# Retention gate columns between the v convolution and the last v transposes, q's norms taken at its convolution, v copied unscaled

## The chip, the cores and the metric

The kernel runs on one core of one Trainium2 chip. The metric is the device time of one execution in microseconds, as the median of several runs. Five engines work beside each other, each through its own list of instructions in order: TensorE (PE; its weight loads are shown apart as PEld), VectorE (DVE), ScalarE (ACT), GpSimd (POOL) and SyncE (SP), which does nothing but issue transfers. ACT issues transfers as well (shown as ACTq). An instruction that waits holds up all that stand behind it on its engine.

## What is computed

One layer of a diffusion backbone on 1024 latent tokens and 256 context tokens, model width 1024. An adaLN-modulated RMSNorm is followed by one input projection, whose columns feed two mixers: a bidirectional gated DeltaNet with four heads and a centred short convolution on q, k and v, and a bidirectional retention with four heads. Their gated outputs go through one output projection and a SwiGLU. The parts that the change touches:

```python
def l2_normalize(t):
    return t * lax.rsqrt(jnp.sum(t * t, axis=-1, keepdims=True) + NORM_EPS)
...
    qkv_a, z, ab, rq, rk, rv, rg = jnp.split(p, splits, axis=-1)
    qkv_a = jnp.concatenate([short_conv(qkv_a[:, :CTX_LEN], cw), short_conv(qkv_a[:, CTX_LEN:], cw)], axis=1)
    q, k, v = [t.reshape(b, tl, N_HEADS_GDN, HEAD_DIM) for t in jnp.split(qkv_a, 3, axis=-1)]
    q = l2_normalize(q) * (HEAD_DIM ** -0.5)
    k = l2_normalize(k)
...
    o_f = gated_delta_rule(q, k, v, g_f, jax.nn.sigmoid(b_f))
...
    o_gdn = rms_norm(o_f + o_b, gdn_norm_g) * jax.nn.silu(z.reshape(b, tl, N_HEADS_GDN, HEAD_DIM))
...
    o_ret = head_group_norm(r_f + r_b, ret_norm_g) * jax.nn.silu(rg.reshape(b, tl, N_HEADS_RET, HEAD_DIM))
```

Inside `gated_delta_rule`, a triangular system with the matrix I + A is solved for each chunk and head, where A holds the products of k with k, times beta and the decay exp(G_i - G_j).

## The kernel before

**Number format.** Every large matmul is done as three: both operands are split into a high part (`whi`, `hhi`) and the rest (`wlo`, `hlo`), and hi·hi, hi·lo and lo·hi are added in one bank. For weights ACT makes `whi` (L344) and DVE or POOL `wlo` (L345).

**Token-major groups.** `token_major(g, ...)` multiplies the normed tokens with 256 columns of the input projection (`tm`, L371 to L373): for eight latent tiles 8 x 24 = 192 matmuls of 128x256. Groups 6 and 7 are the gate columns rg of the retention; their `finish` is `fin_gate`, a Silu on ACT (L532), and the result `res` is stored for later. Groups 8 and 9 are z. Each group has two pairs of split weights, which live in a pool: W2 for groups 6 and 7, W for z and for the convolutions.

**Convolutions.** `conv_block(b, y, lat)` computes one head of k, q or v, channel by token, in banks `b` (L611 to L613), copies the bank to `u` and, scaled, to `y` on ACT (L614, L615), adds the four shifted terms on DVE (L621), and ends with a Silu on ACT (L624). There are three buffers for `y`. Blocks 4 to 7 are k, 0 to 3 q, 8 to 11 v.

**k.** `kstat` (from L630) turns `y` into token-major tiles, sums the squares of each token into `nk`, takes a reciprocal of it, and stores two scaled copies. The decay row `grow_d`, which the pair stage broadcasts, is turned (`GT`, L595) and stored ahead of the k convolutions.

**Row sums.** `ada_rest(5, h)`, called in the first two convolutions of q, accumulates eight products of adaLN weights (`adaw`, loaded in four transfers into two buffers) in `acc` on DVE (L497, L499), sums them over partitions with one matmul on PE (`gr`, L504), adds the bias (`row`, L505) and stores the row (`grow`, L506). It uses one `acc` and one `row`.

**Pair stage.** `pre(t)`, for each of ten tiles (L702 to L737): `kc` is loaded, PE makes `kk` (L705); for latent tiles `qc` is loaded and transposed (`qt`, L710), ACT sums the squares of each token into `nq` (L712), and PE makes `kq` (L715). For both directions the decay row is loaded (`gw`, L718), POOL masks it (`e`, L722), ACT takes four exps (L726), DVE multiplies into `ut` and `sp` (L730, L732), which are stored.

**Inversion and merge.** `invert(b)`, for batches of four, four and two tiles, loads the `ut` as `yr`, copies it to `L` (ACT L758 and DVE L759), does 31 dependent pairs of a product and a subtraction on DVE (`tmp` L765, `X` L767), and turns the result (`XT`, L769). `merge(b)` (`m`, L807 to L838) follows on PE.

**v.** After each v convolution ten transposes (`vT`, L856) go to three banks; ACT scales each 128x128 tile by a factor of its k norm (`vt`, L859, 40 in all), and stores it.

**Order.** The text of the program is ada and norms, token-major groups 0 and 1 (rv), k, q, gates (groups 6, 7), `solve(0)` and `solve(1)` (each `pre` for its tiles, then `invert`), v, `pre` for the last two tiles, merges, z, the scans, and later the rotary groups of the retention. A scheduler that simulates a timeline decides the order on each engine; so z groups and merges are mixed, and the v convolutions run among the pair stage.

Of the kernel before, what the change touches and what calls it, by code (L numbers as in the profile page):

```python
# [17 lines left out]
P = 128  # L18
D = 1024
KT = D // P  # L20
NCTX = 256
# [17 lines left out]
def build(nc, tc, ap, dbg=None, stop=None, marks=None):  # L39
# [151 lines left out]
    try:  # L191
# [402 lines left out]
        ps = bank_b("GT")  # L594
        T.transpose(ps[:80, :P], sm["G"], ident)  # L595
        gT = AB.tile([80, P], F32, tag="gT", name="gT")
        V.tensor_copy(gT, ps[:80, :P])
        SY.dma_start(grow_d, gT)
# [30 lines left out]
        a4, b4, kds4 = (sm[n].rearrange("p (t d h) -> p t d h", d=2, h=4) for n in ("ab", "beta", "kds"))  # L629

        def kstat(h, y):
# [9 lines left out]
            V.tensor_scalar(nk[:, :, h], nk[:, :, h], EPS, None, ALU.add)  # L641
            rk2 = R2.tile([P, TT], F32, tag="rk2", name="rk2", bufs=2)
            V.reciprocal(rk2, nk[:, :, h])
            V.tensor_tensor(a4[:, :, :, h], b4[:, :, :, h], bc(rk2, [P, TT, 2], 2), ALU.mult)
            V.tensor_tensor(kds4[:, :, :, h], kds4[:, :, :, h], a4[:, :, :, h], ALU.mult)
            for (t0, n), pt, kt in zip(cut, ps, kts):
# [21 lines left out]
        nkf = nk.rearrange("p t h -> p (t h)")  # L668

        lnk = log(GS, nkf, TT * H, "ln").rearrange("p (t h) -> p t h", h=H)  # L670
        nG4 = sm["nG"].rearrange("p (t d h) -> p t d h", d=2, h=H)
        V.tensor_tensor(lnb, lnb, bc(lnk, [P, TT, 2, H], 2), ALU.subtract)
# [12 lines left out]
        checkpoint("q")  # L685
        for g in (6, 7):
            token_major(g, LAT, fin_gate, S, W2, SY)
# [12 lines left out]
        def pre(t):  # L700
# [5 lines left out]
            if t >= 2:  # L706
                qc = load(GP, qd[t - 2], "qc", 2)
                pn = bank_b("qt")
                for h in range(H):
                    T.transpose(pn[:, h * P:(h + 1) * P], qc[:, h, :], ident)  # L710
                for h in range(H):
                    S.activation(pn[:, h * P:(h + 1) * P], pn[:, h * P:(h + 1) * P], AF.Square, accum_out=nq[:, t - 2, h:h + 1])  # L712
# [135 lines left out]
        solve(0)  # L848
        solve(1)
        for h in range(H):  # L850
            y = newy()
            conv_block(8 + h, y, False)
# [802 lines left out]
```

## Time and profile before

| what | us |
|---|---|
| median of three runs (1477.37 to 1480.02) | 1479.93 |
| the profiled execution | 1477.96 |
| span of its trace | 1476.2 |
| PE busy | 1397.2 |
| DVE busy | 964.6 |
| ACT busy | 614.0 |
| POOL busy | 590.3 |

The mean clock that was granted to TensorE is 0.983. The span is cut in stages by time below: a row of such a table gives from and to, the length, then the busy time of PE, PEld, DVE, ACT and POOL with the number of instructions in brackets, the granted clock (1.00 is full), the DMA share and GB/s. A row of a timeline gives the start, the length, the engine and the line with its operation, and in brackets the idle time before it and what ended it. A row of grouped instructions ends in busy time and mean ns of one, then the idle time of the engine just before them and its releasers. A row of waits gives the instruction that waited, what it waited for, the total in us, how often, and the longest.

### The profile page before, as it was taken

Reading aid. Unit: us, or ns where it says so; the run is one execution under the profiler, and the core shown is the slowest. Engines: PE = TensorE matmul, PEld = TensorE weight load, DVE = VectorE, ACT = ScalarE, POOL = GpSimd, SP = SyncE. Lnnn points to the kernel's source line nnn. Section 1 sums busy time; section 2 is a strip of 40 time slices with the busy share of each in tenths; the row PEclk is TensorE's granted clock in tenths of the full one; section 3 lists DMA queues with packets and bytes.
Section 4 is the critical chain, followed back from the end, with each engine's and each line's share of the span. In section 5 each row is a group of like instructions: output and inputs, shape, how many; then the busy total and the mean of one; then the engine's idle time right before and its main releaser. Section 6 shows DMA issues by size and latency. Waiting matters only on the chain.

```text
span 1476.2 us, 24111 instructions
## 1 busy us (share of the span) xinstructions
PE 1397.2 (95%) x8919; PEld 1199.2 (81%) x8919; DVE 964.6 (65%) x1856; ACT 614.0 (42%) x1326; POOL 590.3 (40%) x501
## 2 busy tenths in 40 slices
PE   7999999986789999899799899999999999999997
PEld 2898888975689999898688688877888888788885
DVE  6566789289792435689676877556555564657477
ACT  5643564587333111245443623233333332444445
POOL 0120010243202344234144688898555552335321
PEclk9999999998899999999899999999999999999999
DMA  9536686688888625996532265674222242776863
GB/s 337 197 105 205 189 249 200 219 264 277 282 216 277 238 76 178 416 341 209 184 125 104 97 238 210 242 264 162 105 97 105 107 151 79 260 260 194 288 216 114
DMA packets 170421, 298.14 MB, mean 202 GB/s; under 512 B 43496, under 2 KB 93880, under 8 KB 165952
## 3 DMA queue, kind: packets, MB, share of 16 engines
q1 hardware_dynamic: 118752, 253.17, 50.2%
q10 hardware_dynamic: 49072, 35.83, 7.8%
q0 software_dynamic: 2480, 7.60, 1.4%
q8 instruction: 70, 1.15, 0.3%
q14 instruction: 47, 0.39, 0.1%
HBM read 206.60 MB, written 89.96 MB: 201 GB/s over the span
## 4 chain that ended last, share of the span: by engine, by line
PE 55%; POOL 6%; DMA 5%; DVE 4%; issue 2%; ACT 2%; SPq 1%; ACTq 0%; POOLq 0%; DVEq 0%
PE ffn L1344 7%; PE ffn L1342 6%; PE ffn L1343 6%; PE fo L1470 4%; PE fo L1469 4%; PE fo L1468 4%; PE tm L371 3%; PE tm L373 3%; PE tm L372 3%; PE op L1203 2%; PE op L1201 2%; PE op L1202 2%; DMA wd<-tw 2%; POOL ws L1315 1%; DMA pk<-sd 1%
## 5 line engine op out<-in xcount | busy, mean ns | idle before, releaser
L371 PE MATMUL tm<-whi,hhi 128*128 128x256 f32 (+1 forms) x704 | 199.5, 287 | 7.7 <-ACT vt L859 3.4
L372 PE MATMUL tm<-wlo,hhi 128*128 128x256 f32 (+1 forms) x704 | 199.3, 285 | 2.4 <-issue 2.0
L373 PE MATMUL tm<-whi,hlo 128*128 128x256 f32 (+1 forms) x704 | 197.7, 285 | 0.0
L371 PEld LDWEIGHTS tm<-whi,hhi 128*128 128x128 f32 x704 | 132.8, 190 | 11.8 <-ACT vt L859 3.6
L1342 PE MATMUL ffn<-t,whi 128*128 128x512 f32 x352 | 136.9, 390 | 1.3 <-ACT whi L344 1.3
L1344 PE MATMUL ffn<-t,wlo 128*128 128x512 f32 x352 | 137.0, 390 | 1.0 <-DVE wlo L345 1.0
L1343 PE MATMUL ffn<-t,whi 128*128 128x512 f32 x352 | 137.0, 389 | 0.0
L372 PEld LDWEIGHTS tm<-wlo,hhi 128*128 128x128 f32 x704 | 133.7, 190 | 2.1 <-issue 0.9
L373 PEld LDWEIGHTS tm<-whi,hlo 128*128 128x128 f32 x704 | 132.8, 190 | 2.6 <-issue 1.8
L344 ACT ACTIVATE whi<-wraw 128x512 fp32r<-128x512 f32 (+2 forms) x98 | 75.1, 771 | 141.4 <-PE ffn L1343 80.5
L344 ACT ACTIVATE whi<-ws 128x512 fp32r<-128x512 f32 x88 | 55.6, 632 | 171.5 <-PE ffn L1343 123.4
L345 DVE TENSOR_TENSOR wlo<-ws,whi 128x512 fp32r<-128x512 f32 x88 | 93.9, 1068 | 47.0 <-ACT whi L344 46.8
L1469 PE MATMUL fo<-wlo,ahi 128*128 128x512 f32 x308 | 120.2, 390 | 2.1 <-DVE wlo L345 2.1
L1468 PE MATMUL fo<-whi,ahi 128*128 128x512 f32 x308 | 119.3, 390 | 0.7 <-ACT ahi L344 0.7
L1470 PE MATMUL fo<-whi,alo 128*128 128x512 f32 x308 | 119.0, 390 | 0.0
L345 DVE TENSOR_TENSOR wlo<-wraw,whi 128x512 fp32r<-128x512 f32 (+2 forms) x92 | 99.4, 1082 | 24.6 <-ACT whi L344 24.6
L1342 PE MATMUL ffn<-b,whi 128*128 128x512 f32 x264 | 103.8, 393 | 4.4 <-ACT whi L344 4.4
L1344 PE MATMUL ffn<-b,wlo 128*128 128x512 f32 x264 | 103.6, 393 | 0.8 <-DVE wlo L345 0.8
L1343 PE MATMUL ffn<-b,whi 128*128 128x512 f32 x264 | 103.4, 392 | 0.0
L612 PE MATMUL b<-hlo,whi 128*128 128x512 f32 (+1 forms) x256 | 94.4, 369 | 0.0
L613 PE MATMUL b<-hhi,wlo 128*128 128x512 f32 (+1 forms) x256 | 94.3, 368 | 0.0
L611 PE MATMUL b<-hhi,whi 128*128 128x512 f32 (+1 forms) x256 | 94.3, 368 | 0.0
(446 smaller groups left out, 3448.1 us busy)
## 6 DMA issues: line engine op xcount, KB each, us to landing
adaw<-ada SPq DMA_DIRECT2D x48, 512.0 KB, 4.4
pk<-sd SPq DMA_DIRECT2D x16, 1536.0 KB, 10.0
wraw<-wfi SPq DMA_DIRECT2D x44, 512.0 KB, 3.7
ar<-ad SPq DMA_DIRECT2D x33, 512.0 KB, 4.7
w<-wfo SPq DMA_DIRECT2D x22, 512.0 KB, 5.7
wd<-tw SPq DMA_DIRECT2D x11, 1024.0 KB, 4.8
ad<-act SPq DMA_DIRECT2D x20, 512.0 KB, 3.0
raw<-wd SPq DMA_DIRECT2D x20, 512.0 KB, 4.9
```

Source lines behind the costliest of these rows:

```text
L344: S.activation(hi, raw, AF.Copy)
L345: e.tensor_tensor(lo, raw, hi.bitcast(F32), ALU.subtract)
L371: T.matmul(o, hhi[:, k, tsl], whi[:, k % 4, :], start=(k == 0), stop=False)
L372: T.matmul(o, hhi[:, k, tsl], wlo[:, k % 4, :], start=False, stop=False)
L373: T.matmul(o, hlo[:, k, tsl], whi[:, k % 4, :], start=False, stop=(k == KT - 1))
L612: T.matmul(o, whi[:, k, :], hl, start=False, stop=False)
L1342: T.matmul(o, whi[:, k, :], xhi(xn, slice(0, 4), k), start=(first and k == 0), stop=False, **kw)
L1343: T.matmul(o, whi[:, k, :], xlo(xn, slice(0, 4), k), start=False, stop=False, **kw)
L1344: T.matmul(o, wlo[:, k, :], xhi(xn, slice(0, 4), k), start=False, stop=(k == 3), **kw)
L1468: T.matmul(po[g][i], ahi[:, ts], whi, start=(j == 0 and not kw), stop=False, **kw)
L1469: T.matmul(po[g][i], ahi[:, ts], wlo, start=False, stop=False, **kw)
L1470: T.matmul(po[g][i], alo[:, ts], whi, start=False, stop=(j == FH - 1), **kw)
```

## The change

Half of the rg columns (group 7) leave their place ahead of the pair stage and stand between the last v convolution and its transposes; their weights come from pool W. Each head's `vT` follows the next head's convolution (`vturn`), and the copies of v are plain, one for a bank. So that v needs no factor, the norms are arranged anew: `kstat` takes a rsqrt (`rk1`) where it took a reciprocal, and scales `neG` with it too; `grow_d` becomes G less half the log of the squared norm and moves behind that log; the rsqrt of all k norms (`sv`) goes; `rn`, the reciprocal of the squared k norms, enters the output gate with one more product. The squares of q are taken from `y` at the convolutions (`qstat`), no longer in `pre`.

```diff
@@ -595,5 @@
-        ps = bank_b("GT")
-        T.transpose(ps[:80, :P], sm["G"], ident)
-        gT = AB.tile([80, P], F32, tag="gT", name="gT")
-        V.tensor_copy(gT, ps[:80, :P])
-        SY.dma_start(grow_d, gT)
@@ kstat @@
-            V.tensor_scalar(nk[:, :, h], nk[:, :, h], EPS, None, ALU.add)
-            rk2 = R2.tile([P, TT], F32, tag="rk2", name="rk2", bufs=2)
-            V.reciprocal(rk2, nk[:, :, h])
-            V.tensor_tensor(a4[:, :, :, h], b4[:, :, :, h], bc(rk2, [P, TT, 2], 2), ALU.mult)
+            nkh = R2.tile([P, TT], F32, tag="nkh", name="nkh", bufs=2)
+            V.tensor_scalar(nkh, nk[:, :, h], EPS, None, ALU.add)
+            rk1 = rsqrt(R2, nkh, TT, "rk")
+            V.tensor_tensor(a4[:, :, :, h], b4[:, :, :, h], bc(rk1, [P, TT, 2], 2), ALU.mult)
             V.tensor_tensor(kds4[:, :, :, h], kds4[:, :, :, h], a4[:, :, :, h], ALU.mult)
+            V.tensor_tensor(neG4[:, :, :, h], neG4[:, :, :, h], bc(rk1, [P, TT, 2], 2), ALU.mult)
@@ k, q and gates @@
+        V.tensor_scalar(nkf, nkf, EPS, None, ALU.add)
         lnk = log(GS, nkf, TT * H, "ln").rearrange("p (t h) -> p t h", h=H)
+        V.tensor_scalar(lnk, lnk, 0.5, None, ALU.mult)
+        V.tensor_tensor(Gr, sm["G"].rearrange("p (t d h) -> p t d h", d=2, h=H), bc(lnk, [P, TT, 2, H], 2), ALU.subtract)
+        ps = bank_b("GT")
+        T.transpose(ps[:80, :P], Gr.rearrange("p t d h -> p (t d h)"), ident)
+        V.tensor_copy(gT, ps[:80, :P])
+        SY.dma_start(grow_d, gT)
...
-        sv = rsqrt(GS, nkf, TT * H, "sv")
-        V.tensor_tensor(sv, sv, nkf, ALU.mult)
-        sv3 = sv.rearrange("p (t h) -> p t h", h=H)
+        V.reciprocal(rn.rearrange("p t h -> p (t h)"), nkf)
+        def qstat(h, y):
+            for l0 in (0, 4):
+                pn = bank_b("qt")
+                for i in range(4):
+                    T.transpose(pn[:, i * P:(i + 1) * P], y[:, NCTX + (l0 + i) * P:NCTX + (l0 + i + 1) * P], ident)
+                for i in range(4):
+                    S.activation(pn[:, i * P:(i + 1) * P], pn[:, i * P:(i + 1) * P], AF.Square,
+                                 accum_out=nq[:, l0 + i, h:h + 1])
         for h in range(H):
             y = newy()
             conv_block(h, y, True)
...
+            qys.append(y)
+            if h:
+                qstat(h - 1, qys[h - 1])
-        for g in (6, 7):
-            token_major(g, LAT, fin_gate, S, W2, SY)
+        token_major(6, LAT, fin_gate, S, W2, SY)
+        qstat(H - 1, qys[H - 1])
@@ pre @@
-                pn = bank_b("qt")
-                for h in range(H):
-                    T.transpose(pn[:, h * P:(h + 1) * P], qc[:, h, :], ident)
-                for h in range(H):
-                    S.activation(pn[:, h * P:(h + 1) * P], pn[:, h * P:(h + 1) * P], AF.Square, accum_out=nq[:, t - 2, h:h + 1])
@@ v @@
+        def vturn(h, y):
             for t0, n in ((0, 2), (2, 4), (6, 4)):
...
-                for t in range(n):
-                    S.activation(vt[:, t], ps[:, t * P:(t + 1) * P], AF.Copy, scale=sv3[:, t0 + t, h:h + 1])
+                S.activation(vt[:, :n], ps[:, :n * P].rearrange("p (t j) -> p t j", j=P), AF.Copy)
...
+        for h in range(H):
+            ys.append(newy())
+            conv_block(8 + h, ys[h], False)
+            if h:
+                vturn(h - 1, ys[h - 1])
+        token_major(7, LAT, fin_gate, S, W)
+        vturn(H - 1, ys[H - 1])
@@ output gate @@
+            V.tensor_tensor(nqe, nqe, rn[:, l + 2, :], ALU.mult)
```

The order of the instructions changes with it; rows of the order now have the changed kernel's line numbers (`vT` L865, `kk` L723, `kq` L728, Silu of y L619, exps L739). On PE at the end of the q stage, the second row sum of `ada_rest` (`gr`, L504) stood 151 rows behind the first, among the matmuls of group 7. Its surroundings before:

```order
L612 MATMUL b_2376<-hlo,whi 128x512
L613 MATMUL b_2376<-hhi,wlo 128x512
L611 MATMUL b_2376<-hhi,whi 128x512
L504 MATMUL gr<-acc,ones 1x512
L612 MATMUL b_2376<-hlo,whi 128x512
...
L372 MATMUL tm<-wlo,hhi 128x256
L504 MATMUL gr<-acc,ones 1x512
L371 MATMUL tm<-whi,hhi 128x256
```

and now, on the same engine at the same place, behind the convolutions of q (`GT` is the turned decay row, `b_3374` the first bank of v):

```order
L673 MATMUL GT<-ident,Gr 80x128
L504 MATMUL gr<-acc,ones 1x512
L371 MATMUL tm<-whi,hhi 128x256
L372 MATMUL tm<-wlo,hhi 128x256
L373 MATMUL tm<-whi,hlo 128x256
...
L504 MATMUL gr<-acc,ones 1x512
L686 MATMUL qt<-ident,y 128x128 x16
L606 MATMUL b_3374<-hhi,whi 128x256
```

Between the two row sums stand nine matmuls of group 6 where 150 instructions stood, and behind the second come the transposes of q and then v without group 7.

On SP at the same place, the transfers between the two rows keep their order (`grow` are the stored rows, `adaw` and `row` the loads of the second sum, `kc` and `gw` those of the pair stage); `grow_d` is new there:

```order
L676 DMA grow_d<-gT 80x128
L506 DMA grow_1231<-row 1x512
L495 DMA adaw_2305<-ada 128x1024
L503 DMA row<-adarow 1x512
L495 DMA adaw_2309<-ada 128x1024
L506 DMA grow_1231<-row 1x512
L660 DMA kc<-sd 128x512
L731 DMA gw<-grow_d 128x512 x2
```

The loads of the pair stage thus stand behind both stored rows, as they did before, and now behind the decay row too.

On PE around the last ten `vT`, before:

```order
L613 MATMUL b_3980<-hhi,wlo 128x512
L705 MATMUL kk<-kc 128x128 x3
L856 MATMUL vT<-ident,y 128x128 x10
L705 MATMUL kk<-kc 128x128
L710 MATMUL qt<-ident,qc 128x128 x4
L715 MATMUL kq<-qc,kc 128x128 x4
...
L856 MATMUL vT<-ident,y 128x128 x10
L371 MATMUL tm<-whi,hhi 128x256
```

and now, from the last bank of v (`b_3766`) on, where the `tm` ahead of the last `vT` are those of group 7 (48, 120 and 24 in the three gaps) and the one behind it is the first of group 8:

```order
L608 MATMUL b_3766<-hhi,wlo 128x512
L865 MATMUL vT<-ident,y 128x128 x7
L728 MATMUL kq<-qc,kc 128x128 x4
L865 MATMUL vT<-ident,y 128x128 x3
L723 MATMUL kk<-kc 128x128 x4
L371 MATMUL tm<-whi,hhi 128x256
...
L728 MATMUL kq<-qc,kc 128x128 x4
L723 MATMUL kk<-kc 128x128
...
L723 MATMUL kk<-kc 128x128 x3
L728 MATMUL kq<-qc,kc 128x128 x4
...
L865 MATMUL vT<-ident,y 128x128 x10
L371 MATMUL tm<-whi,hhi 128x256
```

The last transposes stood right behind the pair matmuls of their time; now group 7 stands ahead of them. On ACT the Silu of group 7 (L532) and of v (L619) stand among the exps of the pair stage (L739), each with a load of its table where the function changes:

```order
L739 ACTIVATE e<-e,nG 128x128 x4
...
L532 ACT_TABLE_LOAD
L532 ACTIVATE res<-tm 128x256
...
L739 ACT_TABLE_LOAD
L739 ACTIVATE e<-e,nG 128x128 x4
...
L619 ACT_TABLE_LOAD
L619 ACTIVATE y<-y 128x1280
L532 ACTIVATE res<-tm 128x256
```

In the whole program the table loads on ACT go from 20 to 28.

More of the change, by code (lines that the diff above doesn't have):

```diff
@@ L627, in newy @@
             return CV.tile([P, NTOK], F32, tag="y", name="y", bufs=3)
-        a4, b4, kds4 = (sm[n].rearrange("p (t d h) -> p t d h", d=2, h=4) for n in ("ab", "beta", "kds"))
+        a4, b4, kds4, neG4 = (sm[n].rearrange("p (t d h) -> p t d h", d=2, h=4) for n in ("ab", "beta", "kds", "neG"))
         def kstat(h, y):
@@ L846, in solve @@
             checkpoint("inv%d" % b)
[L848 to L852, printed above, removed]
+        def vturn(h, y):
             for t0, n in ((0, 2), (2, 4), (6, 4)):
@@ L857, in build @@
                 vt = CV.tile([P, 4, P], F32, tag="vt", name="vt", bufs=2)
-                for t in range(n):
-                    S.activation(vt[:, t], ps[:, t * P:(t + 1) * P], AF.Copy, scale=sv3[:, t0 + t, h:h + 1])
+                S.activation(vt[:, :n], ps[:, :n * P].rearrange("p (t j) -> p t j", j=P), AF.Copy)
                 S.dma_start(vd[t0:t0 + n, :, h, :].rearrange("t p j -> p t j"), vt[:, :n])
+        solve(0)
+        solve(1)
+        ys = []
+        for h in range(H):
[5 more added lines that the diff above has]
+        vturn(H - 1, ys[H - 1])
         close(CV)
```

4 lines of the change are left out of this document (added).

## The prediction

> **What bounds the kernel now.** I read the shares of the engines first, then the busy time of each engine by stage, then TensorE's waits in the stages that the change touches.
>
> ```profile
> PE 1397.2 (95%) x8919; PEld 1199.2 (81%) x8919; DVE 964.6 (65%) x1856; ACT 614.0 (42%) x1326; POOL 590.3 (40%) x501
> ```
>
> TensorE (PE) is busy for 1397.2 of 1476.2 us. The change leaves the number and the size of its matmuls as they were, so it can win only from PE's 79 us of idle time and from its clock. Next the stages, as from:to, length, then the busy us of PE, weight load, DVE, ACT and POOL, the granted clock, the DMA share, GB/s:
>
> ```profile
> 220.00:262.00 42.00, 42.00 (x242) 35.24 (x241) 39.72 (x81) 18.06 (x44) 2.89 (x2) 1.00 0.62 195
> 262.00:276.00 14.00, 14.00 (x119) 13.94 (x118) 0.00 (x0) 6.56 (x14) 1.27 (x2) 1.00 0.63 189
> 276.00:310.00 34.00, 33.62 (x205) 29.00 (x205) 18.86 (x23) 25.68 (x69) 13.43 (x17) 1.00 0.80 255
> 310.00:375.00 65.00, 44.08 (x261) 37.88 (x259) 60.89 (x89) 54.08 (x155) 29.05 (x23) 0.90 0.84 265
> 375.00:416.00 41.00, 33.22 (x549) 32.21 (x550) 33.27 (x87) 12.30 (x28) 4.67 (x4) 0.96 0.92 271
> 490.00:580.00 90.00, 90.00 (x769) 89.85 (x768) 38.34 (x120) 9.84 (x12) 39.67 (x78) 1.00 0.42 155
> ```
>
> 220 to 276 (q convolutions and gate columns) and 490 to 580 are full. From 276 to 416 PE is idle for 0.4 + 20.9 + 7.8 = 29.1 us, while DVE has nothing at all to do from 262 to 276. This is a stage bound by DVE from 310 on (60.9 of 65) and by PE before it. Its waits, from 276 to 490 (total, times, longest):
>
> ```profile
> PE vT L856 <- ACT y L624: 9.6, 2, 9.3
> PE kk L705 <- issue: 8.4, 3, 6.7
> PE m L814 <- issue: 3.4, 2, 2.2
> PE tm L371 <- ACT vt L859: 3.4, 1, 3.4
> ```
>
> The three places at which group 7 and the plain copies can tell are the last transposes of v (9.3), the copies of v (3.4) and the pair stage (kk, 8.4). The row of the longest (start, length, x count, in brackets the idle time ahead of it and what ended it), an undisturbed one of the same ten transposes, and two rows of the clock, in the columns of the stages, show what it costs besides:
>
> ```profile
> 375.06 2.39 PE L856 MATMUL vT<-ident,y 128*128 128x128 f32 x10 [9.27 <-ACT y L624]
> 305.00 1.31 PE L856 MATMUL vT<-ident,y 128*128 128x128 f32 x10 [0.32 <-ACT y L624]
> ...
> 370.00:375.00 5.00, 0.00 (x0) 0.00 (x0) 5.00 (x7) 4.97 (x12) 3.36 (x2) 0.50 0.48 175
> 375.00:380.00 5.00, 4.95 (x29) 4.95 (x30) 4.52 (x15) 1.77 (x7) 1.18 (x1) 0.66 1.03 355
> ```
>
> In the 5 us after the wait 4.95 us of matmuls ran at 0.66, so about 4.95 x 0.34 = 1.7 us went to the clock. I put the loss of the whole stage (0.90 over 44.1 us of matmuls, part of it transposes) at 3 us. With the 3.4 us of m behind it, PE loses 29.1 + 3.4 + 3 = **35.5 us** here.
>
> **The change, part by part.**
>
> *Group 7's 192 matmuls move from 240–276 to between the v convolutions and the last vT.* They are 22.8 us (192 at the 0.12 us by which the starts of these rows follow each other):
>
> ```profile
> 378.50 0.28 PE L371 MATMUL tm<-whi,hhi 128*128 128x256 f32 x1
> 378.62 0.28 PE L372 MATMUL tm<-wlo,hhi 128*128 128x256 f32 x1
> ```
>
> They fill the 9.3 us ahead of the last vT and part of the 8.4 us at kk. But in their old place they filled something too, which is what is late next. The rows of the adaLN accumulation at the end of the q stage:
>
> ```profile
> 240.21 0.67 DVE L505 TENSOR_TENSOR row<-row,gr 1x512 f32<-1x512 f32 x1
> 243.93 0.33 SPq L495 DMA_DIRECT2D adaw<-ada  x1
> DMA to landing us min/median/max: 3.4/3.9/4.4
> 260.04 1.02 PE L504 MATMUL gr<-acc,ones 128*1 128x512 f32 x2
> 261.10 0.68 DVE L505 TENSOR_TENSOR row<-row,gr 1x512 f32<-1x512 f32 x1 [1.84 <-PE gr L504]
> ```
>
> Between the first row sum and the second lies a chain: SP issues the last weights (adaw) 243.93 - 240.21 = 3.7 us after the first row, behind a DMA that waits for that row; landing takes 3.9; two accumulations of 0.7 follow. That is 9.0 us. Before, some 20 us of matmuls stood between the two gr matmuls and PE did not notice. In the new order there are nine (1.1 us), so PE, which works in order, stands there for about 8.4 us (6 to 11: the ends of the landing row, and the transposition GT just ahead), and by the clock rows above loses 2 us more after it. The Trainium skill, "TensorE: Matmul & The Clock Gate", in its part on transposes, says that transposes do not count as busy for the clock; 16 of them follow this gap, and by that rule the loss would be nearer 3 us. The ten vT that took 2.39 us behind the long wait and 1.31 us elsewhere fit it, but do not prove it.
>
> Where is the second gr then? It was at 260.0 with about 65 of group 7's matmuls (7.7 us) done before it; those are gone and 8.4 us of standing take their place, so it stays at about 261. The kc loads of the pair stage are queued on SP behind the DMA of its row, and so the first ut stays near its old place, too. The v convolutions however now begin at 262 instead of 276, 13 us ahead.
>
> *The squares of q* (32 transposes and 32 squares) go from the pair stage to the q convolutions:
>
> ```profile
> L712 ACT ACTIVATE qt<-qt 128x128 f32<-128x128 f32 x32 | 8.7, 271 | 1.1 <-ACT qt L712 0.8
> L712 ACT ACTIVATION_READ_ACCUMULATOR qt<-qt 128x1 f32 x32 | 6.3, 196 | 0.0
> L710 PE MATMUL qt<-ident,qc 128*128 128x128 f32 x32 | 5.3, 294 | 2.6 <-issue 1.9 <-PE kk L705 0.7
> L859 ACT ACTIVATE vt<-vT,svy 128x128 f32<-128x128 f32 x40 | 11.3, 363 | 13.0 <-DMA sd<-vt 11.7 <-PE vT L856 1.3
> L614 ACT ACTIVATE u<-b 128x512 f32<-128x512 f32 x16 | 9.5, 595 | 5.5 <-PE gr L504 3.8 <-PE b L613 1.7
> L726 ACT ACT_TABLE_LOAD x5 | 6.4, 1283 | 0.9 <-ACT res L532 0.8
> ```
>
> 15.0 us leave ACT in the pair stage and fall into 240 to 280, where it has 24 of 42 us free. The last of them release a buffer of y and the banks of the v convolution, so the first ut may come up to 5.5 us later than 277.5; at nothing at the other end, I take **3 us**.
>
> *The copies of v*: 40 in 11.3 us become 12 of at most 0.6 us each (the 512-wide u<-b above): 11.3 - 7.2 = 4 us off ACT. The wait of 3.4 us that PE had for the last of them goes, as I take it; it stays at worst, since the copy still waits for the DMA that empties its buffer (the 11.7 us in its row).
>
> *More table loads.* The gates of group 7 (Silu) now stand between the exps of the pair stage, and the number of table loads in the program goes from 20 to 28: 8 x 1.283 = 10.3 us on ACT, against 15 + 4 us that left it. The group's eight stores are issued by ACT too, and its two weight loads move from SP's queue to ACT's: ten issues of 0.35 us, 3.5 us more there, and SP is freer by two. The neighbours of one table load show that 1.283 us is all of its price, and the last row is an issue:
>
> ```profile
> 323.89 0.62 ACT L735 ACTIVATE gw<-gw 128x512 f32<-128x512 f32 x1
> 324.52 1.28 ACT L624 ACT_TABLE_LOAD   x1
> 325.81 1.27 ACT L624 ACTIVATE y<-y 128x1280 f32<-128x1280 f32 x1
> 387.83 0.35 ACTq L387 DMA_DIRECT2D zd<-res  x1
> ```
>
> The Trainium skill, "ScalarE: Activation LUTs", section "What ACT_TABLE_LOAD costs", speaks against the change: it has 1283 ns for the load and 1380 ns for a drain, 2.66 us for a switch, and asks that functions be grouped by table set. By that price the eight would be 21 us. The trace agrees with the 1283 ns and shows no drain (0.01 us on either side).
>
> *Small operations of DVE* (a rsqrt for each head of k, Gr, rn, one more in each gate, against a rsqrt of 40 columns that goes) are some 45 more. At the length of a like one now that is 45 x 0.168 = 8 us, spread from the k convolutions to the row sums.
>
> ```profile
> L641 DVE TENSOR_SCALAR nk<-nk 128x10 f32<-128x10 f32 x2 | 0.3, 168 | 0.0
> ```
>
> DVE is busy for 39.7 of 42 us from 220 to 262, so their cover is PE's own full work there and the last y of q, which the new order puts behind the row sums. With the cover they cost nothing, which I take; without it the 8 us would come at GT, and the range has 3 of them.
>
> *Weights of z group 8.* Group 7 now holds the two buffers of the weights until its last matmul, and the low halves of group 8 stand on DVE around the copy XT(0). On PE the matmuls of group 8 come right behind the last vT.
>
> ```profile
> 277.48 1.29 DVE L730 TENSOR_TENSOR ut<-kk,e 128x512 f32<-128x512 f32 x2 [15.70 <-POOL X L755]
> 381.01 2.20 DVE L769 COPY XT<-X 128x1024 f32<-128x1024 f32 x1
> 374.11 0.68 DVE L732 TENSOR_TENSOR sp<-kq,e 128x512 f32<-128x512 f32 x1
> L730 DVE TENSOR_TENSOR ut<-kk,e 128x512 f32<-128x512 f32 x20 | 13.5, 685 | 30.9 <-POOL X L755 15.7 <-ACT e L726 7.0 <-DMA un<-ut 4.4
> 389.32 0.20 DVE L765 TENSOR_TENSOR tmp<-L,X 128x31 f32<-128x31 f32 x1 [5.03 <-ACT L L758]
> 404.21 0.58 PE L807 MATMUL m<-t,U 32*32 32x32 f32 x4
> 276.29 1.95 PE L705 MATMUL kk<-kc 128*128 128x128 f32 x16
> ```
>
> When is XT(0)? From the first ut to its end (277.5 to 383.2, 105.7 us) DVE worked 18.9 + 60.9 + 8.2 = 88 us. Its idle time before 310 waited for PE's convolutions, which are 13 us ahead now; I leave it only the 4.1 us of 310 to 375: 277.5 + 3 + 88.0 + 4.1 = **372.6**, 10.6 us sooner. When does PE reach the last vT? From 276.3 to 375.1 it worked 98.8 - 21.3 = 77.5 us; with 22.8 more for group 7, 5 less for the transposes of q, and 4 us of waits at kk (between none and the 8.4 of now; half), from 262 on: 361.3, and 363 with the vT. The low halves are there at about 370.4, ahead of the XT copy, so PE waits some **7.4 us** (1, if the halves were free to come at once).
>
> **The sum**, twice. On PE: 35.5 us lost before; after it 8.4 + 2 at the row sums, 4 at kk, 7.4 at group 8, 3.4 at m, together 25.2: a gain of 10.3. On DVE: XT(0) 10.6 us sooner; the merge began at 404.2, 21 us after it, and would begin at 393.6. From there on the work is as before. The profiled run took 1477.96 us (2 under the median, 1479.93), and so I say **1468**.
>
> **The rivals.**
>
> *More goes.* The waits at kk and for group 8 don't come (0 and 1), as the pair stage gets its operands earlier and its ACT is relieved by 19 - 10.3 - 3.5 = 5 us: 35.5 - 10.4 - 1 - 3.4 = 20.7 us, and 24 if the m waits go too: 1457 to 1454. For it: DVE's 14 idle us from 262. Against it: the first ut is where it was.
>
> *Nothing comes of it.* The pair stage has a pace of its own: its 20 steps ran from 277.5 to 374.8, 4.86 us each, through exp, select, product and DMA. If it keeps that, XT(0) comes 3 us later and the last vT's wait merely turns into one for the weights or at kk; the 5.0 us for L (ACT stood behind the DMA of the vt copies) are saved: about -2, **1476**. For it: POOL and DMA (0.84) had part in the pace. Against it: DVE was full from 310 on, with work that now comes sooner.
>
> *Slower.* The switches of tables lie in the path of the exps, each of which releases a ut: 3 + 10.3 - 5.0 = +8.3, **1486**. It decides as soon as what was added (10.3) isn't met by what left ACT in the same steps, so that the 10.9 us that ACT had free from 310 to 375 are used up; the order on ACT puts gates that wait for PE's group 7 ahead of exps, which is for it, and the 19 us that left are against it. With the page's 2.66 us it would be +19.
>
> **How the numbers follow.** My forecast (1462 to 1473) 0.45; more 0.17; nothing 0.14; slower 0.24, with the gap at the row sums at its upper end in it. 0.2%, about what a measurement of this kernel tells from no change, is 3 us: faster 0.62, same 0.14, slower 0.24. The range goes from 1450 (more, with the kk waits and clock all gone) to 1486.
>
> **What would show it.** Right: a PE wait of about 8 us at the second gr L504, ended by DVE's acc; no long wait ahead of the last vT; XT(0) near 373, merge near 394; eight more table loads of 1283 ns with ACT still under 60 of 65. Wrong: a first ut after 283, no wait at gr, ut waits for e of more than the 7 us of now, or a merge at or after 404.

## The result and the profile after

The changed kernel takes 1493.49 us (median, 1489.83 to 1495.77); the kernel before took 1479.88 us in the same comparison. The ratio is 1.0096, with a 95% interval of 1.0075 to 1.0117: 13.6 us slower, where 10 us faster was forecast. The profiled execution has a span of 1493.9 us against 1476.2.

The first row of the page after, to be held against that of before:

```profile
PE 1405.3 (94%) x8919; PEld 1206.9 (81%) x8919; DVE 978.4 (65%) x1900; ACT 619.7 (41%) x1306; POOL 592.9 (40%) x501
```

The same 8919 matmuls took 8.1 us more of PE's time (1405.3 against 1397.2), and PE was idle for 88.6 us instead of 79.0. Of the 17.7 us in the span, 9.6 are idle time and 8.1 the longer time of the same matmuls; the mean granted clock was 0.972 against 0.983. The stages, in the columns of the table of before:

```profile
220.00:262.00 42.00, 33.53 (x189) 27.17 (x187) 30.83 (x75) 16.35 (x56) 4.45 (x5) 0.88 0.66 200
276.00:310.00 34.00, 32.12 (x199) 29.00 (x198) 22.69 (x26) 25.54 (x65) 14.82 (x13) 0.95 0.83 267
310.00:375.00 65.00, 58.32 (x393) 52.81 (x392) 59.85 (x100) 49.31 (x95) 23.14 (x22) 0.97 0.87 270
375.00:416.00 41.00, 28.98 (x198) 27.90 (x198) 24.37 (x58) 11.81 (x19) 5.94 (x5) 0.79 0.86 267
416.00:490.00 74.00, 60.82 (x1373) 57.31 (x1371) 38.01 (x95) 22.52 (x42) 4.00 (x7) 0.86 0.67 186
```

The last of them had been nearly full before:

```profile
416.00:490.00 74.00, 70.56 (x1231) 67.71 (x1231) 38.92 (x106) 18.78 (x36) 12.55 (x25) 0.98 0.82 244
```

From 310 to 375 PE stood still for 6.7 us where it had stood for 20.9: this is the part that the change aimed at, and it worked. The idle time came back in three places: 8.5 us in 220 to 262, where there had been none, 12.0 instead of 7.8 in 375 to 416, and 13.2 instead of 3.4 in 416 to 490. In the last two the granted clock fell to 0.79 and 0.86. The waits of PE in 276 to 490, summed by line (us, count, longest):

```profile
PE tm L371 <- ACT res L532: 11.5, 3, 6.8
PE m L830 <- issue: 7.5, 2, 4.6
PE vT L865 <- ACT res L532: 5.1, 2, 4.2
```

and the one at the row sums, from PE's timeline:

```profile
256.69 1.86 PE L504 MATMUL gr<-acc,ones 128*1 128x512 f32 x2 [8.20 <-DVE acc L499]
```

The wait of 9.3 us ahead of the last vT is 4.2 now. That for the row sum is 8.20 us, where 8.4 was forecast. New are the waits for `res`; the merges' own (`m`) have grown from 4.3 us to 11.0.

What the merge waits for is seen on ACT, SP and DVE (start, length, engine, operation, count). After:

```profile
374.12 0.68 ACT L739 ACTIVATE e<-e,nG 128x128 f32<-128x128 f32 x2
374.82 1.28 ACT L532 ACT_TABLE_LOAD   x1
376.12 0.38 ACT L532 ACTIVATE res<-tm 128x256 f32<-128x256 f32 x1
376.52 1.28 ACT L739 ACT_TABLE_LOAD   x1
377.81 0.40 ACT L739 ACTIVATE e<-e,nG 128x128 f32<-128x128 f32 x1
378.30 0.69 DVE L743 TENSOR_TENSOR ut<-kk,e 128x512 f32<-128x512 f32 x1 [3.15 <-ACT e L739]
381.46 1.06 DVE L782 COPY XT<-X 128x1024 f32<-128x1024 f32 x1
392.87 2.94 SPq L796 DMA_DIRECT2D U<-un  x2
408.00 0.33 SPq L891 DMA_DIRECT2D rope<-rope  x1
408.42 4.83 SPq L801 DMA_DIRECT2D t<-xd  x4
417.13 0.25 PE L820 MATMUL m<-t,U 32*32 32x32 f32 x6
422.83 1.07 DVE L782 COPY XT<-X 128x1024 f32<-128x1024 f32 x1
426.85 0.67 DVE L823 TENSOR_SCALAR xt<-m 128x512 f32<-128x512 f32 x1
```

and the same places before:

```profile
375.45 0.51 SPq L783 DMA_DIRECT2D U<-un  x1
391.78 0.56 SPq L783 DMA_DIRECT2D U<-un  x1
393.59 10.27 SPq L788 DMA_DIRECT2D t<-xd  x4
409.58 0.68 DVE L810 TENSOR_SCALAR xt<-m 128x512 f32<-128x512 f32 x1
415.24 1.09 DVE L769 COPY XT<-X 128x1024 f32<-128x1024 f32 x1
```

XT of batch 0 stands where it stood (381.5 against 381.0), but the merge begins 12.9 us later (417.1 against 404.2). Two things differ. The two loads `U<-un` of 2 MB each left SP 16 us apart and now leave together, after XT; and `xt`, the first merge's negated copy, stood ahead of XT of batch 1 on DVE and now stands behind it.

### The profile page after: what moved, and what is told of

Same layout as the page of the kernel before. It is cut to its first block, busy times and chain, and to the rows that moved or that the text cites. A ratio compares the mean times of both kernels' runs of the same rounds, so it can differ in the third digit from the quotient of the medians.

```text
span 1493.9 us, 24143 instructions
## 1 busy us (share of the span) xinstructions
PE 1405.3 (94%) x8919; PEld 1206.9 (81%) x8919; DVE 978.4 (65%) x1900; ACT 619.7 (41%) x1306; POOL 592.9 (40%) x501
## 4 chain that ended last, share of the span: by engine, by line
PE 51%; DMA 8%; POOL 6%; DVE 5%; issue 3%; ACT 2%; SPq 0%; ACTq 0%; DVEq 0%; POOLq 0%
PE ffn L1364 6%; PE ffn L1363 6%; PE ffn L1362 6%; PE fo L1488 4%; PE fo L1490 4%; PE fo L1489 4%; PE tm L371 2%; PE tm L373 2%; PE tm L372 2%; PE op L1221 2%; PE op L1223 2%; PE op L1222 2%; POOL ws L1335 1%; DMA wd<-tw 1%; DMA w<-wfo 1%
## 5 line engine op out<-in xcount | busy, mean ns | idle before, releaser
L371 PE MATMUL tm<-whi,hhi 128*128 128x256 f32 (+1 forms) x704 | 203.8, 293 | 16.1 <-ACT res L532 11.5
L372 PE MATMUL tm<-wlo,hhi 128*128 128x256 f32 (+1 forms) x704 | 203.0, 290 | 0.5 <-DVE wlo L345 0.5
L373 PE MATMUL tm<-whi,hlo 128*128 128x256 f32 (+1 forms) x704 | 201.2, 290 | 0.0
L371 PEld LDWEIGHTS tm<-whi,hhi 128*128 128x128 f32 x704 | 136.8, 196 | 21.2 <-ACT res L532 12.2
L372 PEld LDWEIGHTS tm<-wlo,hhi 128*128 128x128 f32 x704 | 137.6, 195 | 2.2 <-issue 0.9
L373 PEld LDWEIGHTS tm<-whi,hlo 128*128 128x128 f32 x704 | 136.8, 196 | 0.7 <-DVE hlo L314 0.2
## 6 DMA issues: line engine op xcount, KB each, us to landing
pk<-sd SPq DMA_DIRECT2D x16, 1536.0 KB, 10.4
```

The costliest lines, as they stand in the source:

```text
L371: T.matmul(o, hhi[:, k, tsl], whi[:, k % 4, :], start=(k == 0), stop=False)
L372: T.matmul(o, hhi[:, k, tsl], wlo[:, k % 4, :], start=False, stop=False)
L373: T.matmul(o, hlo[:, k, tsl], whi[:, k % 4, :], start=False, stop=(k == KT - 1))
```

## The experiments

Each run is compared with runs of the kernel before on the same chip (1478 to 1481 us); the ratio to those and its interval are given. Where the trace is used, these are its milestones: the first ut, XT of batch 0, the first `U<-xd` on SP, the first matmul of merge 0 and of merge 2 (start, us), and the span.

```
kernel       first ut   XT 0    U<-xd   merge 0  merge 2   span
before         277.48  381.01  403.89   404.21   457.38  1476.2
after          277.88  381.46  413.30   417.13   478.37  1493.9
e1_rope        277.76  381.52  409.23   416.29   473.64  1493.0
e5_copy        278.33  378.96  408.06   410.87   470.91  1486.0
e3_g7back      279.15  383.05  406.12   407.91   470.41  1488.3
e4_g7only      270.55  376.73  409.45   406.70   467.40  1489.3
p_qstat        283.26  387.72  411.10   412.75   471.39  1489.9
p_vturn        279.58  381.92  406.25   406.99   465.03  1485.9
p_norm         279.79  383.36  406.53   406.65   466.00  1483.1
e6_ada         282.91  384.55  417.95   421.74   481.56  1495.7
e8_rope_u1     278.15  381.98  406.08   408.87   468.78  1486.2
e11_u1_xt      278.06  383.68  405.49   409.92   468.27  1481.0
b_jam          277.83  383.08  404.33   401.30   462.40  1485.7
e14_copy       277.78  378.32  401.94   405.55   464.36  1477.1
e15_row2       266.58  368.05  396.06   399.49   460.89  1474.4
e21_b_row2     259.08  380.51  403.58   408.81   462.87  1481.1
```

In all of them the span ends 1012 to 1023 us behind the first matmul of merge 2. So what delays the merges delays the end, to within some 10 us.

**1. Is it the rope table on SP?** It waits from 395.8 to 408.0 with the merge's loads behind it. It is put behind mk[0], the last U<-xd of merge 0.

```diff
         merge(0)
-        SY.dma_start(rope, ap["rope"])
+        with tc.issue_after(mk[0]):
+            SY.dma_start(rope, ap["rope"])
```

> The changed kernel with one transfer moved on SP: the load of the rope table is queued behind the merge's own loads of batch 0 and no longer ahead of them. Theory A (a convoy of transfers: the rope load waits on SP until 408 for a store of v that lands late, and the merge's loads stand behind it): the t loads start near 396 where they started at 408.4, the first merge matmul comes at 404 to 408 where it came at 417, and the kernel takes 1480 to 1486 us. Theory B (the queues are simply full until 408, whatever stands first): the t loads land no sooner, the merge stays at 415 or later, 1491 to 1496 us. Theory C (table loads of group 7 on ScalarE set the end): no effect, 1491 to 1496 us.

1494.10 us, 1.0093 (1.0066 to 1.0120). The t loads were issued at 396.0, 12 us sooner, as theory A had it, but `U<-xd` left at 409.2 and merge 0 began at 416.3. Theory A falls: the rope table stood in a queue that moved no faster without it. Theories B and C had both expected this time.

**2. Is it the table loads?** The Silu of group 7 is left out: fin_copy is fin_gate with a plain copy in its place.

```diff
-        token_major(7, LAT, fin_gate, S, W)
+        token_major(7, LAT, fin_copy, S, W)
```

> The changed kernel with a plain copy in place of the Silu for the gates of group 7 (the Silu of half of the retention gates is left out); the order of the instructions stays the same, six of the eight added table loads go. Theory C (table loads in the path of the exps and of the gates): XT of batch 0 3 to 6 us sooner than 382.5, TensorE's waits for res fall from 11.5 us to under 5, and 1482 to 1487 us. Theory A (the convoy of transfers): XT a little sooner, the store of v and what hangs on it too, at most 4 us in all: 1489 to 1492 us.

1490.03 us, 1.0070 (1.0047 to 1.0092): 3.5 us of the 13.6, XT 2.5 us sooner. That lies in the range of theory A, which e1_rope rules out, and above that of theory C. The intervals of this run and of the changed kernel overlap, so the table loads are a part of the loss at most.

**3. Which part of the change costs?** The whole without the move of group 7 (e3_g7back), and four parts, each alone on the kernel before.

```diff
 e3_g7back (on the changed kernel)
-        token_major(6, LAT, fin_gate, S, W2, SY)
+        for g in (6, 7):
+            token_major(g, LAT, fin_gate, S, W2, SY)
-        token_major(7, LAT, fin_gate, S, W)
 e4_g7only: token_major(7, ..., S, W) ahead of the last head's transposes, nothing else
 p_qstat: qstat at the q convolutions, nothing else
 p_vturn: vturn(h - 1) behind conv_block(8 + h), copies scaled, nothing else
 p_norm: rk1, Gr, rn and plain copies, nothing else
```

> The changed kernel with group 7 back ahead of the pair stage; the norms, the plain copies and the later turning of v stay. Theory A and C (the move of group 7 is what costs): no wait at the second row sum, XT and merge as before the change or sooner, 1472 to 1481 us. Theory D (the rest of the change costs: the squares of q, the decay row behind the k norms, more small VectorE work): 1485 us or more, with a first ut later than 278.

1490.94 us, 1.0069 (1.0048 to 1.0090), with the first ut at 279.2, as theory D expected.

> The kernel before with only group 7 moved between the last v convolution and its transposes. Theory A and C: as slow as the whole change, 1488 to 1496 us, with the stores of v landing late and ten more table loads. Theory E (the gap at the row sums, which needs the squares of q moved as well: here 115 instructions stand between the two sums where nine stood): no wait at the row sum, and 1478 to 1484 us.

1491.04 us, 1.0073 (1.0053 to 1.0093), in the range of theories A and C. Yet the first ut and XT came 6.9 and 4.3 us sooner than in the kernel before. In the merges PE waited 8.4 us for the loads `t<-xd` and 6.1 us for ACT's `t`.

> The kernel before with one part alone: the squares of q taken at the convolutions. With group 7 back in its place the rest of the change cost 10 us; theory D1 (the squares of q, which fill ScalarE and TensorE ahead of the pair stage, cost it): 1487 to 1491 us, first ut after 278.5. Theory D2 (the norms cost it) and D3 (the later turning): within 3 us of the kernel before, 1478 to 1483.

1492.04 us, 1.0082 (1.0044 to 1.0120), just above the range of theory D1; the first ut is 5.8 us late and XT 6.7.

> The kernel before with one part alone: each head of v is turned after the next head's convolution, copies still scaled. Theory D3 (turned later, the stores of v come later and run into the loads of the merge): 1486 to 1491 us, the merge at 407 or later. Theory D1 and D2: within 3 us of the kernel before.

1487.94 us, 1.0064 (1.0040 to 1.0087), as theory D3 expected; XT is only 0.9 us late, merge 0 2.8.

> The kernel before with one part alone: v unscaled with plain copies, and what that takes (a rsqrt for each head of k, the decay row behind the k norms, rn in the output gate); squares of q, turning of v and group 7 as before. Theory D2 (more small VectorE work and a later decay row hold up the end of the q stage): 1486 to 1491 us, first ut after 279. Theory D1 and D3: 1475 to 1482, since ScalarE has 28 copies fewer.

1482.48 us, 1.0031 (1.0014 to 1.0047), between the two ranges.

Every part costs, and the four add up to 2.5%, where the whole costs 0.96%. So none of them is "the" cause, and the costs overlap. In each of the four merge 2 begins 7.7 to 14.0 us later than before, so the merges are probably where they are paid; no run separates this. With group 7 moved, 28 to 33 us lie between XT and the first `U<-xd` (after, e1, e4, e5, e6); where it is in its place, 23 to 24 (before, e3 and the three p runs). That points to the two big loads, which group 5 tests. They can't be all of it: in e4_g7only one of them left SP only at 412.7, behind the merge's loads, and the distance is 32.7 us all the same.

**4. Does the gap at the row sums matter?** The last two sums are accumulated beside the first ones.

```diff
         for g in range(2):
             ada_rest(2, g)
+            ada_rest(5, g)
...
-            if h < 2:
-                ada_rest(5, h)
```

> The changed kernel with the last two adaLN row sums accumulated early, beside those of the rv columns, and no longer in the convolutions of q. Theory G (the gap of 8.2 us at the second row sum, with the slow clock behind it, is a fixed part of the loss): no wait at the row sums, PE idle from 240 to 262 under 1 us, first ut at 268 to 272, and 1480 to 1485 us. Theory H (what sets the end is the chain from the pair stage through the inversions to the merges, which fills whatever the front gives it): the gap goes, first ut comes sooner, but XT of batch 0 stays at 378 or later and the kernel at 1489 to 1495 us.

1496.10 us, 1.0128 (1.0093 to 1.0162). The wait at gr is gone, but the first ut came at 282.9, 5 us later, and PE waited 6.9 us for the convolution's banks and 4.3 for kc instead. Theory G's first ut didn't come; the run says nothing of a shorter chain in its old place.

**5. Are the merge's transfers and its xt the loss?** On the changed kernel, U of batch 1 and the rope table are queued behind the merge's loads (e8_rope_u1); with xt on ACT as well (e11_u1_xt). On the kernel before, the cost put in: U of batch 1 behind that of batch 0 (b_jam). And a control, the kernel before with xt on ACT and the rope table later (e13_best_b).

```diff
-            SY.dma_start(uu..., un[b])
+            with tc.issue_after(mk[0]) if b else nullcontext():
+                SY.dma_start(uu..., un[b])
...
-            V.tensor_scalar(xt1..., ps1..., -1.0, None, ALU.mult)
+            S.activation(xt1..., ps1..., AF.Copy, scale=-1.0)
```

> The changed kernel with two transfers moved on SP: the 2 MB load of U for batch 1 and the rope table are queued behind the merge's loads of batch 0. Theory J (with group 7 moved, the load of U for batch 1 no longer leaves ahead of XT but beside the 2 MB load of batch 0, and the merge's small loads land behind both): the loads U<-xd start at 404 to 408 where they started at 413.3, the first merge matmul comes at 406 to 411 where it came at 417.1, and the kernel takes 1483 to 1488 us. Theory K (the load is only paid later): merge 0 is sooner, but merge 1 still starts at 449 to 452, and 1491 to 1496 us.

1486.89 us, 1.0048 (1.0031 to 1.0064): 6.6 us back. On its SP queue and on its DVE:

```profile
395.03 0.33 SPq L798 DMA_DIRECT2D U<-un  x1
395.72 10.26 SPq L803 DMA_DIRECT2D t<-xd  x4
406.08 3.07 SPq L802 DMA_DIRECT2D U<-xd  x4
410.13 0.52 SPq L798 DMA_DIRECT2D U<-un  x1
412.33 0.69 DVE L825 TENSOR_SCALAR xt<-m 128x512 f32<-128x512 f32 x1
417.21 1.03 DVE L783 COPY XT<-X 128x1024 f32<-128x1024 f32 x1
```

`U<-xd` leaves 7.2 us sooner and merge 0 begins 8.3 sooner. With the merge sooner, xt stands ahead of XT of batch 1 again. In e1_rope, where the rope table alone is moved, it still stands behind it (424.4 against 422.0), so it is the load of U that brings this about.

> The kernel before with the suspected cost put in: the 2 MB load of U for batch 1 is queued behind that of batch 0 (it stood ahead of XT). Theory J: U<-xd starts 5 to 9 us later than 403.9, the merges too, and the kernel takes 1484 to 1490 us. Theory K: within 2 us of the kernel before, since that load is not needed before merge 1.

1486.64 us, 1.0044 (1.0028 to 1.0061): the inserted cost alone is 7.5 us. The expected later issue doesn't come (404.3 against 403.9), nor a later first matmul of merge 0 (401.3 against 404.2); what comes later is the landing. U of batch 1 left SP at 403.7, right ahead of the small loads, 17 us behind U of batch 0; three loads `yr<-un` of 64 KB each had moved there too. One of PE's waits there:

```profile
PE m L816 <- DMA U<-xd: 7.4, 1, 7.4
```

The 0.9 us that PE waited for this load before are 7.4. The Trainium skill, "DMA: Bandwidth & Descriptors", section on queues, rings and completion order, says that each transfer engine takes the descriptors of a ring in order. The small loads behind the 2 MB, for which PE waited 7.4 us, agree with it.

> As e8_rope_u1, and the negated copy xt of the first merge product is taken by ScalarE, where VectorE did it in its queue behind XT of batch 1. Theory L (xt behind XT of batch 1 costs 4 us more than before the change): m<-U,xt comes within 7 us of m<-t,U and not 10.5, and the kernel is 3 to 6 us faster than e8_rope_u1, 1478 to 1484 us. Rival: ScalarE stands in waits for the stores of z, and nothing is won: the same as e8_rope_u1 within 2 us.

1481.97 us, 1.0017 (1.0001 to 1.0033): another 4.9 us, as a number what theory L expected. But m<-U,xt comes 6.6 us after m<-t,U in e8_rope_u1 already and 6.5 in e11_u1_xt, and merge 2 only 0.5 us sooner: of the 5.2 us between the spans, 4.7 lie behind the first matmul of merge 2 (1012.7 us to the end against 1017.4). So it isn't the start of the merges that xt's move mends, as theory L had it. The traces show where the gain arises: the scan's first `up` comes at 495.4, against 494.9 in e8_rope_u1, and the last one at 666.2 against 668.8; the first `ffn` comes 3.6 us sooner. How xt's move brings that about is not shown.

> The kernel before with xt on ScalarE and the rope table behind the merge's loads; nothing else. There xt already stands ahead of XT of batch 1, so theories J and L expect a gain of 0 to 3 us, 1476 to 1480 us. If any new order costs by itself what the single parts cost (5 to 12 us, whatever is edited), it takes 1484 us or more.

1479.42 us, 0.9996 (0.9980 to 1.0013): xt on ACT and the later rope table are worth nothing to the kernel before, where U of batch 1 leaves early as it is.

**6. Where is the gain that was forecast?** All on e11_u1_xt: without table loads (e14_copy); with two buffers for the row sums (e15_row2); with group 7 back (e12_u1_xt_g7); with the norms alone (e16_norm).

```diff
 e15_row2
-            acc = R2.tile([P, 512], F32, tag="acc", name="acc", bufs=1)
+            acc = R2.tile([P, 512], F32, tag="acc", name="acc", bufs=2)
-                row = R2.tile([1, 512], F32, tag="row", name="row", bufs=1)
+                row = R2.tile([1, 512], F32, tag="row", name="row", bufs=2)
```

> As e11_u1_xt, with a plain copy in place of the Silu for the gates of group 7 (the Silu of half of the retention gates is left out); same order, six table loads fewer. If the table loads hold up the last exps: XT of batch 0 3 to 4 us sooner than 383.7 and the kernel at 1477 to 1480 us. If they lie beside other waits: within 1.5 us of 1482.

1477.50 us, 0.9987 (0.9973 to 1.0001): 4.5 us for six table loads (7.7 us), in one and the same order. The ut that ended last, in e11_u1_xt and then in e14_copy:

```profile
380.52 0.69 DVE L743 TENSOR_TENSOR ut<-kk,e 128x512 f32<-128x512 f32 x1 [3.06 <-ACT e L739]
383.68 1.08 DVE L783 COPY XT<-X 128x1024 f32<-128x1024 f32 x1
```

```profile
375.60 0.68 DVE L743 TENSOR_TENSOR ut<-kk,e 128x512 f32<-128x512 f32 x1
378.32 1.09 DVE L783 COPY XT<-X 128x1024 f32<-128x1024 f32 x1
```

The wait of 3.06 us for the exp is gone, and XT is 5.4 us sooner, more than the 3 to 4 that were expected.

> As e11_u1_xt, with two buffers each for the accumulator and the row of the row sums (the chain between the two sums is then shorter by the wait for the row's buffer); the new order has three instructions between the sums and the last pair matmuls ahead of most of group 7. If the gap and the late pair matmuls kept XT of batch 0 in place: the gap is under 5 us, the last ut at 370 or sooner, XT at 372 to 377, and 1472 to 1478 us, faster than the kernel before. If the pair stage's own pace (exp, mask, product, transfers) sets XT: the gap shrinks but XT stays within 3 us of 382, and 1479 to 1485 us.

1475.95 us, 0.9983 (0.9965 to 1.0001): 6.0 us faster than e11_u1_xt and by the median 3.8 faster than the kernel before, though the interval just reaches no change. Its row sums, first ut and XT:

```profile
245.62 1.02 PE L504 MATMUL gr<-acc,ones 128*1 128x512 f32 x2
247.01 1.02 PE L504 MATMUL gr<-acc,ones 128*1 128x512 f32 x2
266.58 1.29 DVE L743 TENSOR_TENSOR ut<-kk,e 128x512 f32<-128x512 f32 x2 [5.33 <-PE kk L723]
368.05 1.12 DVE L783 COPY XT<-X 128x1024 f32<-128x1024 f32 x1
```

No wait stands at the second sum, the pair stage starts 11.5 us sooner than in e11_u1_xt, and XT comes 15.6 us sooner: past what was forecast for the change itself. As the order changed too (the last pair matmuls now stand ahead of most of group 7), the run doesn't say how much of this is the row sums'. Merge 0, however, comes only 10.4 us sooner than there, and merge 2 3.5 us later than in the kernel before.

> As e11_u1_xt, with group 7 back ahead of the pair stage. If the loss of the rest of the change (1490.9 with group 7 back) is the same order of the merge's loads and of xt: 1479 to 1484 us. If it is the squares of q ahead of the pair stage: 1487 us or more.

1486.53 us, 1.0044 (1.0029 to 1.0059): above the first range and just under the second. With group 7 in its old place the two mends bring 4.4 us, not 11.5.

> Only the norms and the plain copies of v (squares of q, turning of v and group 7 as before), with U of batch 1 and the rope table behind the merge's loads and xt on ScalarE. That part alone took 1482.5 us; with the two mends 1475 to 1480 if the merges follow sooner, 1481 to 1484 if its cost lies in the q stage.

1481.07 us, 1.0012 (0.9996 to 1.0028): the norms under the mends are level with the kernel before.

**7. Does that gain need group 7 in its new place, and can the Silu go elsewhere?** The kernel before with the two row buffers, xt on ACT and the rope table later (e21_b_row2); e15_row2 with the gates of group 7 stored raw, loaded in the z stage, put through the Silu and stored again (e20_late2).

> The kernel before with the mends alone: two buffers each for accumulator and row, xt on ScalarE, the rope table behind the merge's loads; group 7 and all else as before. If the gain of e15_row2 comes from the row sums alone: 1474 to 1477 us. If it needs group 7 in its new place, since only there the shorter chain lets the pair stage start sooner: 1478 to 1482 us, first ut within 3 us of 277.5.

1483.05 us, 1.0022 (1.0007 to 1.0038). The first ut came at 259.1, 18 us sooner than before, and XT at 380.5, 0.5 us sooner. Neither was expected like this: the time lies above both ranges, and the first ut was to stay near 277.5. DVE shows why the early start is lost:

```profile
279.35 2.40 DVE L621 SCALAR_TENSOR_TENSOR y<-u,cw,y 128x254 f32<-128x254 f32 x4 [18.99 <-ACT y L615]
```

It stood 19.0 us for the copy of the first bank of the v convolutions, which PE computes only behind group 7. With group 7 ahead, an early start of the pair stage is not worth anything; in e15_row2, with group 7 behind the convolutions, XT came sooner with the first ut.

> As e15_row2, with the gates of group 7 stored raw and their Silu taken in the z stage (each tile loaded, passed through the Silu and stored again by GpSimd's queue); four table loads fewer in the program, the order on TensorE in the pair stage is the same. If the table loads cost here what they cost in e14_copy: 1471 to 1474 us, XT of batch 0 at 364 to 367. If the eight loads and stores in the z stage collide with the merges: 1476 us or more.

1504.09 us, 1.0169 (1.0146 to 1.0193). XT stays at 368.2 and merge 2 at 460.5, but the eight loads and stores cost 27 us behind them: PE waits 8.1 us in the scan (`up` for ACT's `vn`) and 7.1 us for `res`. As a way to save table loads it is none. Nor does it bear out e14_copy's price: ACT has 12 table loads from 240 to 385 where e15_row2 has 18, and XT comes no sooner (368.2 against 368.1).

## Why the prediction was wrong, step by step

- **The row sums** (8.4 us of standing, 2 of clock, first ut about 280.5): right. 8.20 us, and the first ut at 277.9, though the second sum came at 256.7 and not at about 261. PE's 5.04 us of work after it ran at 0.61, which is 2.0 us and not the 3 of the other estimate:

```profile
256.60:262.00 5.40, 5.04 (x19) 2.97 (x19) 0.68 (x1) 2.30 (x12) 0.00 (x0) 0.61 0.20 63
```

  Three slips of the working change nothing here: 9.0 less 1.1 is 7.9, not 8.4; 192 times 0.12 is 23.0; and the 24 us that ACT had free are those of 220 to 262.
- **The last vT and kk**: the waits were nearly right. 4.2 us were left at the last vT, for ACT's `res`, where none was forecast, and 4.9 at kq, where 4 was forecast at kk. The place was wrong: the last vT ended at 382.6, not at 363. From 262 to there PE worked for 106.9 us and stood for 13.7, where the sum had 95 and 4. It had counted PE's work from 276 on, where 253 of the 288 matmuls of the v convolutions stood; now all 288 stand behind the row sums. So do the 32 transposes of q, which it had taken off.
- **Table loads**: eight more, as forecast, each 1.283 us. That they were met by what left ACT was wrong in this order. e5_copy and e14_copy give 3.5 and 4.5 us for six; two of them stood between the last exps (ACT at 374.82 to 377.81 in the profile), not where ACT was free. A share of busy time (49.3 of 65 us) doesn't show that. In the order of e15_row2 and e20_late2, six fewer moved XT by nothing.
- **XT of batch 0 at 372.6**: the first step that failed. It ended at 382.5. The sum gave DVE only 4.1 us of idle time from the first ut to XT, because its idle time before 310 was put down to PE's convolutions. The trace of the kernel before does not bear that out: from 277.5 to 310 DVE waited for exps (5.1 us), for stores of ut (4.4), for kq (2.0) and 2.1 us for others, but for no convolution. So having the convolutions earlier took none of it away. After the change DVE was idle for 17.8 of 104.7 us from the first ut to the end of XT, against 18.5 of 105.8 before. Its waits there; 6.9 us of the second row lie ahead of the first ut:

```profile
DVE ut L743 <- ACT e L739: 10.1, 6, 3.1
DVE ut L743 <- PE kk L723: 7.4, 2, 6.9
```

  The pair stage kept its pace, as the second rival had it, and of the third rival's table loads 5.4 us are seen at XT (e14_copy). From the first ut to the end of XT the forecast had 92 us; it was 104.6, still 101.6 without the six table loads, and 102.6 in e15_row2. There XT came to 368.1 because the pair stage started sooner, not because DVE waited less. The forecast's mechanism is seen in none of these.
- **"21 us after it" for the merge, and "from there on the work is as before"**: the step that made it slower. The merge began 34.6 us after XT's end. The 2 MB load of U for batch 1, which had left ahead of XT, left beside that of batch 0; that put the merge's small loads back and with them xt behind XT of batch 1 on DVE. e8_rope_u1 takes 6.6 us of it out of the changed kernel, and b_jam puts 7.5 us into the kernel before. e11_u1_xt takes out 11.5, but what it adds lies behind the merges. PE's waits at m, left at 3.4 us in the sum, were 11.0. The big load was in no rival: the third had the right sign and, within 8 us, the size, but a mechanism that explains only a part. That it came nearest is in the main luck.
- **The weights of group 8** (7.4 us): the place was right, the cause not. Behind the last vT PE waited 9.1 us for `res` (the other 2.4 of the 11.5 lie in group 7), as ACT stood 12.6 us for a store of z, with the DMA share at 0.86.

What stays open: why the rest of the change costs some 7 us under the same mends where group 7 is back (e12_u1_xt_g7, 1486.5), while the norms alone cost nothing there; how e11_u1_xt gains over e8_rope_u1 in the scan; why an XT 13 us sooner (e15_row2 against before) brings merge 0 only 4.7 us; and what else keeps the merge's loads back when group 7 moves (e4_g7only). In e15_row2 U of batch 0 leaves SP 18.5 us behind XT, where it was 10.8 before; SP's longest wait ahead of it, 7.5 us, ends with a load of weights (`wraw`).

## What to carry to other kernels

Work that is moved to fill a wait leaves a hole behind and changes when everything after it is queued; the forecast has to follow the next chain to its end, transfers included, and not stop where the wait is filled. A large load that isn't needed yet belongs behind the small ones that are; forcing one such load into a good kernel is a cheap test of what it costs. Where a change turns out slower, one mend alone may show little: here the changed kernel got level with the kernel before, and by the median ahead of it, only with the merge's loads, xt and the row sums put right as well.

## What the runs showed of the hardware

Of the 17.7 us by which the span grew, 8.1 came as the same 8919 matmuls taking longer; the granted clock was 0.79 and 0.86 in the two stages where PE was idle for 29 and 18% of the time. A table load took 1.283 us on ACT. Six of them cost 4.5 us of the kernel's time in one order (e14_copy), and in another six fewer moved XT by nothing (e20_late2). A load of 2 MB right ahead of loads of 128 KB on one queue made PE wait 7.4 us for these, where it had waited 0.9 (b_jam).
